# Mixture of experts: a written TensorE order per expert pair, the scatter a pair later, and six of eight gate units inside the pairs

## The chip, the core and the metric

The kernel runs on one core of a Trainium2 chip. The metric is the device time of one execution in microseconds (us); each kernel is run several times and the median is compared. The engines of the core run side by side, each with its own in-order queue: TensorE (PE, matmuls; its weight loads are PEld), VectorE (DVE), ScalarE (ACT), GpSimd (POOL) and SyncE (SP), which here issues nearly all DMA transfers from memory.

## The reference, cut to what matters

Two blocks run on 512 tokens of 1024 features: first two hybrid attention layers with MLPs, then two layers of the second block. The change is in the second half of a layer of the second block:

```python
for i in range(2):
    mix = even_mixer(x, ...) if i % 2 == 0 else odd_mixer(x, ...)
    x = layer_norm(ALPHA * x + mix @ w_o[i], ln1_g[i], ln1_b[i])
    ffn = expert_choice_moe(x, router_w[i], w1[i], w3[i], w2[i])
    ple = sigmoid(x @ ple_gate_w[i] + ple_gate_b[i]) * (p[i] @ ple_w[i])
    x = layer_norm(ALPHA * x + ffn + ple, ln2_g[i], ln2_b[i])

def expert_choice_moe(x, router_w, w1, w3, w2):   # 16 experts, 64 tokens each
    aff = softmax(x @ router_w)                   # 512 x 16
    gates, idx = top_k(aff.T, 64)
    xg = x[idx]                                   # gather
    hid = silu(xg @ w1) * (xg @ w3)               # w1, w3: 1024 x 1024 per expert
    ye = (hid @ w2) * gates
    return zeros.at[idx].add(ye)                  # scatter
```

All of it is float32. The weights of the experts are 16 x 3 x 4 MB per layer, about 200 MB, and each is used once.

## The kernel before, in words

`K.program` runs the layers; `moe` (L1401) is the second half of a layer of the second block. It first multiplies by w_o, normalizes, and computes the routing (`route_tile`, then `choose`: eight rounds of maximum and replace on DVE, and a running count that gives each token its slot, slT). Beside `choose`, TensorE computes gate units. A gate unit (`ple_unit`, L1571) is 128 of the 1024 features of the ple term: 24 matmuls of the gate (pg), 6 of ple_w (pv), a tanh on ACT, a multiply on DVE, four transposes (pt). Its gate weights are loaded as float32 and split in a high and a low part (whi by ACT, wlo by DVE or POOL). Four units run early, their results wait in the tiles `early`; the other four run later, two in pair 1 and two in pair 2.

`experts` (L1604) handles the 16 experts in 8 pairs. One-hot matrices (OH, of four experts, that is two pairs) come from slT. A gather is 64 matmuls of the token features with OH, for two pairs at once. For each pair, each half (512 columns) of w1 and w3 gives two products a1 and a3 (`pair_product`): 8 matmuls in the program, 16 instructions in the trace (float32 goes in two passes), on half of the array for each expert (128 rows x 64 columns), with two weight chunks of 1 MB. Then silu and multiply (ACT, DVE), four transposes of the hidden half (ht), transposes of the affinities (ot), and four products with w2 (y). yh and yl are the split of y times the gate; the scatter is 16 matmuls (sc) in 8 tiles, each added to the tokens by DVE.

Each pair loads 24 chunks of 1 MB. They go through a ring of slots: three in the pool `wr`, five in r1. A slot is loaded again when the products that read it are done; a late gate weight also takes a slot, until it is split. When the late units are over, their memory (`xfp`, `ple`, `wh`) is closed and a pool r2 of 7 slots (layer 0) or 6 (layer 1) is opened over it, before pair 3. Matrix sizes give the memory per partition: xf 2 x 16 KB, pT 2 x 4 KB, early 4 x 2 KB, then the pool `ple` 6 KB (pw, pwh, pwl, pz) and `wh` 8 KB; r2 is 8 KB per slot.

At the start of pair 0 the tokens are scaled by ln1's gain and bias on POOL (`ln_half`, L1541, tiles lnh): four rows, two tags of one buffer.

The order on each engine is not the program's. A scheduler places the instructions with its own estimate of times, by priority and readiness, and adds the semaphores; each engine and each DMA queue then runs its list in order. So before, TensorE's list mixes the products of one pair with the scatter, the gather, the units and the next pair's products.

PSUM has eight banks: two for a1/a3 (tag a), two for y, two for sc, one each for t (ht, ot) and ga.

## Time and profile before

| | us |
|---|---|
| median of 3 runs | 3537.59 (3535.84 to 3539.7) |
| the profiled execution | 3527.1 |
| its span, first to last instruction | 3525.3 |
| TensorE busy in the span | 3346.5 (95%) |
| DVE / ACT / POOL busy | 1579.2 / 1071.5 / 524.3 |

The profile is one execution of the kernel. Busy time of TensorE is from a model of when matmuls end, and overlaps with waiting, so 95% is not a measure of how near the engine is to its peak. The page cuts the span in 40 slices of 88 us; the two expert stages are slices 25 to 30 and 35 to 40.

### The profile page before, as it was taken

The numbers are of one execution on the slowest core, as the hardware profiler recorded it, in microseconds if no ns is written. First come the engines' busy times: TensorE is split into PE (matmuls) and PEld (weight loads), VectorE is DVE, ScalarE is ACT, GpSimd is POOL, SyncE is SP. The second block draws the span as 40 slices with busy tenths as digits, with TensorE's granted clock in tenths as the row PEclk, the third lists the DMA queues.
The fourth block names the chain that finished last, engine by engine and source line by source line (L and its number), as shares of the span: only waits on it lengthen the run. The fifth ranks groups of instructions, "written<-read, shape, count | busy, mean of one in ns | idle before, by whom it ended". The sixth has DMA issues, their size and how long they took to land. (4 is left out here: it accounts for less than half of the span.)

```text
span 3525.3 us, 37543 instructions
## 1 busy us (share of the span) xinstructions
PE 3346.5 (95%) x15018; PEld 2137.7 (61%) x15018; DVE 1579.2 (45%) x2516; ACT 1071.5 (30%) x1937; POOL 524.3 (15%) x368
## 2 busy tenths in 40 slices
PE   8999999999999999999989789999997998999997
PEld 6666588888766658888856774443335667344332
DVE  6555463445555546344567752122116765112213
ACT  4343333223443333322365431111003543111011
POOL 2012120002001212001221323000003203200001
PEclk9999999999999999999989889999998999999999
DMA  5111032333211103233220226999992113889997
GB/s 182 48 37 59 26 108 87 99 101 124 72 60 37 48 28 104 93 98 96 78 76 3 72 109 264 379 373 421 421 402 79 37 38 117 362 340 421 421 421 297
DMA packets 221279, 584.84 MB, mean 166 GB/s; under 512 B 17328, under 2 KB 158000, under 8 KB 169904
## 3 DMA queue, kind: packets, MB, share of 16 engines
q1 hardware_dynamic: 220672, 581.66, 43.6%
q8 instruction: 118, 1.93, 0.2%
q10 hardware_dynamic: 432, 0.79, 0.1%
q14 instruction: 57, 0.47, 0.0%
HBM read 580.30 MB, written 2.10 MB: 165 GB/s over the span
## 5 line engine op out<-in xcount | busy, mean ns | idle before, releaser
L218 ACT CAST whi<-w 128x1024 fp32r<-128x1024 f32 (+1 forms) x312 | 311.1, 1003 | 733.6 <-PE mm L228 502.0
L1631 PE MATMUL a<-w,xg 128*64 128x512 f32 x2048 | 488.1, 597 | 20.4 <-DMA w<-in_w_dram 17.8
L227 PE MATMUL mm<-h,whi 128*128 128x512 f32 x1056 | 415.9, 394 | 4.6 <-ACT whi L218 4.2
L229 PE MATMUL mm<-h,wlo 128*128 128x512 f32 x1056 | 416.6, 395 | 0.1
L228 PE MATMUL mm<-l,whi 128*128 128x512 f32 x1056 | 414.0, 392 | 0.0
L221 DVE TENSOR_TENSOR wlo<-w,whi 128x1024 fp32r<-128x1024 f32 (+1 forms) x234 | 300.3, 1287 | 211.4 <-ACT whi L218 208.3
L1631 PEld LDWEIGHTS a<-w,xg 128*64 128x64 f32 x2048 | 151.5, 136 | 305.7 <-issue 262.3
L221 POOL TENSOR_TENSOR wlo<-w,whi 128x1024 fp32r<-128x1024 f32 x78 | 173.6, 2228 | 782.9 <-ACT whi L218 688.9
L1631 PE MATMUL y<-w,hT 128*64 128x512 f32 x1024 | 268.2, 599 | 0.0
L227 PEld LDWEIGHTS mm<-h,whi 128*128 128x128 f32 x1056 | 199.4, 189 | 49.7 <-ACT whi L218 5.4
L228 PEld LDWEIGHTS mm<-l,whi 128*128 128x128 f32 x1056 | 199.2, 189 | 46.1 <-issue 0.7
L229 PEld LDWEIGHTS mm<-h,wlo 128*128 128x128 f32 x1056 | 199.3, 189 | 44.2 <-DVE wlo L221 1.0
L602 DVE TENSOR_REDUCE mx<-s 128x1 f32<-128x128 f32 x192 | 93.2, 488 | 190.7 <-PE s L601 189.9
L1631 PEld LDWEIGHTS y<-w,hT 128*64 128x64 f32 x1024 | 76.3, 136 | 136.0 <-issue 128.4
L604 ACT ACTIVATE P<-s,mx 128x128 f32<-128x128 f32 x192 | 100.9, 527 | 174.7 <-DVE mx L602 162.4
L1689 DVE SCALAR_TENSOR_TENSOR th<-th,a 128x512 f32<-128x512 f32 x32 | 22.0, 688 | 291.5 <-ACT th L1688 291.4
L1726 DVE TENSOR_TENSOR xtok<-xtok,sc 128x512 f32<-128x512 f32 x128 | 83.5, 683 | 151.7 <-PE sc L1724 151.7
L948 POOL TENSOR_TENSOR u<-u 128x512 f32<-128x512 f32 x64 | 66.6, 1040 | 521.3 <-ACT E L947 275.5
L1697 POOL TENSOR_TENSOR og<-OH,aff 128x512 f32<-128x512 f32 x16 | 16.8, 1048 | 679.4 <-PE ot L1700 662.8
L959 DVE TENSOR_TENSOR y<-mm,r 128x512 f32<-128x512 f32 x64 | 44.2, 690 | 160.8 <-PE mm L229 160.8
L1688 ACT ACTIVATE th<-a 128x512 f32<-128x512 f32 x32 | 19.1, 597 | 319.1 <-PE a L1631 319.1
L227 PE MATMUL mm<-E,whi 128*128 128x512 f32 x256 | 99.7, 389 | 0.0
(584 smaller groups left out, 6286.8 us busy)
## 6 DMA issues: line engine op xcount, KB each, us to landing
w<-in_w_dram SPq DMA_DIRECT2D x384, 1024.0 KB, 16.8
w<-in_w_in_dram SPq DMA_DIRECT2D x32, 1024.0 KB, 5.3
w<-in_w_up_dram SPq DMA_DIRECT2D x32, 1024.0 KB, 5.5
w<-in_w_down_dram SPq DMA_DIRECT2D x32, 1024.0 KB, 5.1
w<-in_w_out_dram SPq DMA_DIRECT2D x8, 1024.0 KB, 5.0
w<-in_w_o_dram SPq DMA_DIRECT2D x8, 1024.0 KB, 4.7
w<-in_ple_gate_w_dram SPq DMA_DIRECT2D x8, 1024.0 KB, 5.2
w<-in_w_in_even_dram SPq DMA_DIRECT2D x7, 1024.0 KB, 5.5
```

Of the source, the lines that this page charges most:

```text
L218: nc.scalar.copy(h, view)
L221: e.tensor_sub(l, view, h)
L227: mm(ps, wh, xh, start=first, stop=False)
L228: mm(ps, wh, xl, start=False, stop=False)
L229: mm(ps, wl, xh, start=False, stop=last)
L602: nc.vector.tensor_reduce(mx[:, i:i + 1], s[:, :n], axis=X, op=OP.max, negate=True)
L604: nc.scalar.activation(pv, s[:, :n], AF.Exp, bias=mx[:, i:i + 1], accum_out=sums[:, i:i + 1])
L948: nc.gpsimd.tensor_mul(u, u, u)
L959: nc.vector.tensor_mul(y, ps, r2)
L1631: nc.tensor.matmul(ps[64 * a:64 * a + 64], lhs(a, 4 * kc + k), cw[a][:, k], start=kc == 0 and k == 0, stop=kc == 1 and k == 3)
L1689: nc.vector.scalar_tensor_tensor(th, th, 1.0, a1, op0=OP.add, op1=OP.mult)
L1726: nc.vector.tensor_add(xs, xs, ps)
```

## The change

TensorE's instructions of the expert stage get a dependency each on the one before (`keep_order`), so that their order is the program's. In the program, a pair now is: the products with w1 and w3 of both halves; then one block with the transposes of the first hidden half and of og, the first gate unit, the scatter of the pair before (`left`), the unit's transposes, the second unit, in pairs 1, 3 and 5 the gather of the next two pairs, the transposes of the second hidden half and of the second unit; then the products with w2. Only two gate units run early, and pairs 1 to 3 have two each; r2 opens at pair 4. yh, yl, oT and the lnh tags get two buffers, and og and ogT share one. The last pair scatters its first half before the last two chunks' products. The ring's slots are taken in the order two of `wr`, five of r1, one of `wr`.

```diff
...
             self.pT = [fp.tile([128, 2, T], F32R, name=f"pT{a}") for a in "hl"]
-            early = [fp.tile([128, T], F32, name=f"pe{m}") for m in range(4)]
+            early = [fp.tile([128, T], F32, name=f"pe{m}") for m in range(2)]
             with ExitStack() as e2:
...
                         self.side_input(l, p, pp)
-                        pgs = [self.gate_load(self.wr, l, i) for i in range(2)]
+                        pg = self.gate_load(self.wr, l, 0)
                     for t in range(4):
...
                         for m in range(4):
-                            self.ple_unit(l, p, pp, m, pgs[m // 2], "wo", "t", early[m])
+                            if m < 2:
+                                for _ in self.ple_unit(l, p, pp, m, pg, ("wo", "wo"), early[m]):
+                                    pass
                             for h in range(2):
...
+    def keep_order(self, first):
+        nc, tc = self.nc, self.tc
+        prev = None
+        for i in nc.cur_bb.bb.instructions[first:]:
+            if i.engine == nc.tensor.engine:
+                if prev is not None:
+                    tc.add_manual_dep(i, prev.name, mybir.DependencyInfo(mybir.DependencyClass.NoSync, mybir.DependencyReason.DATA),
+                                      reason="keep_order")
+                prev = i
     def ln_half(self, p, l, h, *names):
...
         for a, name in zip("gb", names):
-            t = p.tile([128, 512], F32, name="lnh", tag=name)
+            t = p.tile([128, 512], F32, name="lnh", tag=name, bufs=2)
             nc.sync.dma_start(t, bcast(I[f"ln1_{a}_2"][l][512 * h:512 * h + 512], [[0, 128], [1, 512]]))
...
-    def ple_unit(self, l, p, pp, m, pg, tag, tag2, z=None):
+    def ple_unit(self, l, p, pp, m, pg, tags, z=None):
...
         XF = [[self.xf[a][:, k] for k in range(8)] for a in range(2)]
-        ps = pp.tile([128, T], F32, name="pg", tag=tag)
+        ps = pp.tile([128, T], F32, name="pg", tag=tags[0])
         self.proj(ps, pg[:, :, s], *XF, pool=early)
-        pv = pp.tile([128, T], F32, name="pv", tag=tag)
+        pv = pp.tile([128, T], F32, name="pv", tag=tags[1])
         h, lo = [p.tile([128, 2, 128], F32R, name=f"pw{a}") for a in "hl"]
...
         if not early:
-            z = p.tile([128, T], F32, name="pz")
+            z = p.tile([128, T], F32, name="pz", bufs=1)
         nc.scalar.activation(z, ps, AF.Tanh, scale=0.5, bias=self.pb[:, m:m + 1])
...
             nc.vector.scalar_tensor_tensor(z, z, 1.0, pv, op0=OP.add, op1=OP.mult)
-        pt = pp.tile([128, 4, 128], F32, name="pt", tag=tag2)
+        yield
+        pt = pp.tile([128, 4, 128], F32, name="pt", tag="t", bufs=2 if early else 1)
         for t in range(4):
             nc.tensor.transpose(pt[:, t], z[:, 128 * t:128 * t + 128], C["ident"])
-        if not early:
+        if early:
+            nc.scalar.copy(z.rearrange("p (t f) -> p t f", t=4), pt)
+        else:
             nc.vector.tensor_add(xs, xs, pt)
-            return
-        nc.scalar.copy(z.rearrange("p (t f) -> p t f", t=4), pt)
+        yield
...
             self.wh = ef.enter_context(self.pool("wh", 1, side="right"))
-            cyc = [self.wr] + [r1] * R1 + [self.wr] * 2
+            cyc = [self.wr] * 2 + [r1] * R1 + [self.wr]
             self.nch = 0
...
+            def one_hot(grp):
+                OH = p.tile([128, 4, 4, 64], F32R, name="OH")
+                nc.vector.tensor_tensor(OH, slT[:, :, 4 * grp:4 * grp + 4, None].to_broadcast([128, 4, 4, 64]),
+                                        slot[:, None, None, :].to_broadcast([128, 4, 4, 64]), op=OP.is_equal)
+                return OH
             def gather(xg, OH, k2s):
...
                 for k2 in k2s:
-                    ps = pp.tile([128, 2, 256], F32, name="ga", tag="ga", bufs=1) if grp or k2 % 2 == 0 else pp.tile([128, 2, 256], F32, name="ga", tag="y")
+                    ps = pp.tile([128, 2, 256], F32, name="ga", tag=("ga", "y")[k2 % 2], bufs=1 + k2 % 2)
                     for kk in range(2):
...
+            def hidden(th, half, hT):
+                ps = pp.tile([128, 4, 128], F32, name="ht", tag="t", bufs=1)
+                for k in range(4):
+                    nc.tensor.transpose(ps[:, k], th[:, 128 * k:128 * k + 128], C["ident"])
+                nc.scalar.copy(hT[:, 4 * half:4 * half + 4], ps)
+            def scatter(oT, ys, halves, last=False):
+                for half in halves:
+                    yh, yl = ys[half]
+                    for t in range(4):
+                        ps = pp.tile([128, T], F32, name="sc", tag=("y", "sc")[t // 2])
+                        ts_ = slice(128 * t, 128 * t + 128)
+                        nc.tensor.matmul(ps, oT[:, ts_], yh, start=True, stop=False)
+                        nc.tensor.matmul(ps, oT[:, ts_], yl, start=False, stop=True)
+                        xs = x[:, t, 512 * half:512 * half + 512]
+                        nc.vector.tensor_add(xs, xs, ps)
+                        if last:
+                            self.ln_stats(p, st[:, t], x[:, t], half)
+                            if half and l == 0:
+                                self.ln_norm(p, st[:, t], x[:, t])
+            first = len(nc.cur_bb.bb.instructions)
+            OH = one_hot(0)
+            xg = p.tile([128, 8, 256], F32, name="xg")
+            gather(xg, OH, range(2))
+            left = None
             for pi in range(8):
                 grp, pr = divmod(pi, 2)
-                if pi == 3:
+                if pi == 4:
                     ef.close()
...
                         G, Bb = self.ln_load(es.enter_context(self.pool("lng", 1, side="right")), l, "ln2")
-                if pr == 0:
-                    OH = p.tile([128, 4, 4, 64], F32R, name="OH")
-                    nc.vector.tensor_tensor(OH, slT[:, :, 4 * grp:4 * grp + 4, None].to_broadcast([128, 4, 4, 64]),
-                                            slot[:, None, None, :].to_broadcast([128, 4, 4, 64]), op=OP.is_equal)
-                    xg = p.tile([128, 8, 256], F32, name="xg")
-                    gather(xg, OH, range(2))
                 e0 = 2 * pi
+                og = p.tile([128, 4, 2, 64], F32, name="og")
+                nc.gpsimd.tensor_mul(og, OH[:, :, 2 * pr:2 * pr + 2], aff[:, :, e0:e0 + 2, None].to_broadcast([128, 4, 2, 64]))
+                if pr and pi < 7:
+                    OH = one_hot(grp + 1)
                 hT = p.tile([128, 8, 128], F32, name="hT")
+                ths = []
                 for half in range(2):
...
                     for kc in range(2):
-                        if pr == 0 and half == 0 and kc == 1:
+                        if pi == half == 0 and kc == 1:
                             gather(xg, OH, range(2, 4))
...
                                     nc.gpsimd.tensor_add(xs, xs, Bb)
-                                for m in range(4) if h == 0 else ():
+                                for m in range(2) if h == 0 else ():
                                     xs = x[:, :, 128 * m:128 * m + 128]
...
                     nc.vector.tensor_mul(th, th, a3)
-                    ps = pp.tile([128, 4, 128], F32, name="ht", tag="t", bufs=1)
-                    for k in range(4):
-                        nc.tensor.transpose(ps[:, k], th[:, 128 * k:128 * k + 128], C["ident"])
-                    nc.scalar.copy(hT[:, 4 * half:4 * half + 4], ps)
-
-                og = p.tile([128, 4, 2, 64], F32, name="og")
-                nc.gpsimd.tensor_mul(og, OH[:, :, 2 * pr:2 * pr + 2], aff[:, :, e0:e0 + 2, None].to_broadcast([128, 4, 2, 64]))
+                    ths.append(th)
+                units = []
+                if 0 < pi < 4:
+                    pg = self.gate_load(slot_pool(), l, pi)
+                    units = [self.ple_unit(l, plp, pp, 2 * pi + i, pg, ("sc", ("sc", "y")[i])) for i in range(2)]
+                hidden(ths[0], 0, hT)
                 ps = pp.tile([128, T], F32, name="ot", tag="t", bufs=1)
...
                 gate = p.tile([128, 1], F32, name="gate", bufs=2)
-                ogT = p.tile([128, T], F32, name="ogT", tag="th", bufs=2)
+                ogT = p.tile([128, T], F32, name="ogT", tag="og")
                 nc.scalar.activation(ogT, ps, AF.Copy, scale=0.5, accum_out=gate)
-                oT = p.tile([128, T], F32R, name="oT")
+                oT = p.tile([128, T], F32R, name="oT", bufs=2)
                 nc.vector.tensor_scalar(oT, ogT, 0.0, None, op0=OP.is_gt)
+                for u in units[:1]:
+                    next(u)
+                if left:
+                    scatter(*left, range(2))
+                for u in units:
+                    next(u)
+                if pr and pi < 7:
+                    xg = p.tile([128, 8, 256], F32, name="xg")
+                    gather(xg, OH, range(4))
+                hidden(ths[1], 1, hT)
+                for u in units[1:]:
+                    next(u)
                 if pi == 7:
                     self.exp_ln_table()
+                ys = []
                 for half in range(2):
-                    if pi in (1, 2) and half == 0:
-                        pg = self.gate_load(slot_pool(), l, pi + 1)
-                        for m in (2 * pi + 2, 2 * pi + 3):
-                            self.ple_unit(l, plp, pp, m, pg, "sc", "sc")
                     y = pp.tile([128, T], F32, name="y", tag="y")
...
                         pair_product(y, w2, e0, lambda a, k: hT[:, k, 64 * a:64 * a + 64], half, kc)
-                    yh = p.tile([128, T], F32R, name="yh")
-                    yl = p.tile([128, T], F32R, name="yl")
+                        if pi == 7 and half and kc == 0:
+                            scatter(oT, ys, range(1), True)
+                    yh = p.tile([128, T], F32R, name="yh", bufs=2)
+                    yl = p.tile([128, T], F32R, name="yl", bufs=2)
                     nc.scalar.activation(yh, y, AF.Copy, scale=gate)
                     nc.vector.scalar_tensor_tensor(yl, y, gate, yh, op0=OP.mult, op1=OP.subtract)
-                    for t in range(4):
-                        ps = pp.tile([128, T], F32, name="sc")
-                        ts_ = slice(128 * t, 128 * t + 128)
-                        nc.tensor.matmul(ps, oT[:, ts_], yh, start=True, stop=False)
-                        nc.tensor.matmul(ps, oT[:, ts_], yl, start=False, stop=True)
-                        xs = x[:, t, 512 * half:512 * half + 512]
-                        nc.vector.tensor_add(xs, xs, ps)
-                        if pi == 7:
-                            self.ln_stats(p, st[:, t], x[:, t], half)
-                            if half and l == 0:
-                                self.ln_norm(p, st[:, t], x[:, t])
+                    ys.append((yh, yl))
+                left = oT, ys
+            scatter(*left, range(1, 2), True)
+            self.keep_order(first)
             if l == 1:
...
```

## Rows read from the trace of the kernel before

**Rows 1.** The page: span, and the rate of the transfers in 40 slices.
```profile
span 3525.3 us, 37543 instructions
...
GB/s 182 48 37 59 26 108 87 99 101 124 72 60 37 48 28 104 93 98 96 78 76 3 72 109 264 379 373 421 421 402 79 37 38 117 362 340 421 421 421 297
```

**Rows 2.** Windows of both stages: length, engines' busy time, PEclk, DMA share, GB/s.
```profile
2138.70:2647.80 509.10, 483.15 (x2144) 198.33 (x2144) 101.93 (x153) 55.42 (x97) 35.60 (x29) 1.00 0.95 389
2995.30:3502.20 506.90, 486.92 (x2144) 198.53 (x2144) 101.79 (x153) 55.48 (x97) 35.67 (x29) 1.00 0.94 389
```

**Rows 3.** Windows of 50 us, those with late gate units.
```profile
2250.00:2300.00 50.00, 50.00 (x216) 23.20 (x217) 12.11 (x19) 4.42 (x8) 0.00 (x0) 1.00 0.77 308
2300.00:2350.00 50.00, 49.41 (x227) 23.55 (x224) 10.17 (x14) 7.51 (x12) 3.40 (x2) 1.00 0.92 374
...
3100.00:3150.00 50.00, 50.00 (x214) 24.48 (x213) 11.13 (x17) 6.35 (x11) 1.05 (x1) 1.00 0.87 347
3150.00:3200.00 50.00, 48.51 (x227) 24.60 (x227) 11.20 (x15) 7.39 (x12) 1.05 (x1) 1.00 0.85 352
```

**Rows 4.** Chain of waits at layer 0's first gather: start, us, what.
```profile
2120.99 0.35 PE slp L1538 x4
...
2137.43 1.23 DVE OH L1663
2138.70 4.10 PE ga L1642 x32
```

**Rows 5.** Timeline of TensorE, layer 1: start, us, instruction, [idle before].
```profile
2977.47 0.42 PE L1538 MATMUL slp<-c_ident,cum 16*128 16x16 f32 x4
...
2995.29 0.38 PE L1642 MATMUL ga<-OH,xkh 128*128 128x256 f32 x1 [0.48 <-DVE OH L1663]
```

**Rows 6.** Timeline of DVE, layer 0, after the slots' transposes.
```profile
2121.38 0.22 DVE L1539 TENSOR_SCALAR slT<-slp 128x64 f32<-128x64 f32 x1 [2.34 <-PE slp L1538]
```

**Rows 7.** Timeline of the SP queue, start of both stages.
```profile
2149.89 0.33 SPq L1547 DMA_DIRECT2D lnh<-in_ln_b_dram  x1
2152.18 44.25 SPq L1623 DMA_DIRECT2D w<-in_w_dram  x22
...
3008.76 2.05 SPq L1623 DMA_DIRECT2D w<-in_w_dram  x4
```

**Rows 8.** The loads of expert weights: issue to landing.
```profile
DMA to landing us min/median/max: 4.7/16.8/21.2
```

**Rows 9.** Timeline of TensorE: uncut products, transposes, a cut product.
```profile
2155.11 10.52 PE L1631 MATMUL a<-w,xg 128*64 128x512 f32 x48
2165.56 0.66 PE L1693 MATMUL ht<-c_ident,th 128*128 128x128 f32 x4
...
2190.30 1.07 PE L1631 MATMUL y<-w,hT 128*64 128x512 f32 x2
```

**Rows 10.** Timeline of TensorE: an early unit's first matmul, and what follows the unit.
```profile
2113.75 0.50 PE L227 MATMUL pg<-xfh,whi 128*128 128x512 f32 x1 [1.59 <-ACT pe L1593]
...
2120.93 0.42 PE L1538 MATMUL slp<-c_ident,cum 16*128 16x16 f32 x4
```

**Rows 11.** TensorE's waits in the first stage: total us, times, longest.
```profile
PE ot L1700 <- ACT hT L1694: 2.3, 3, 0.8
```

**Rows 12.** DVE operations of scatter and unit: ns minimum, median, maximum.
```profile
L1726 DVE TENSOR_TENSOR xtok<-xtok,sc x61: 672/686/689, 2192.3 to 2650.0; 128x512 f32<-128x512 f32 x61
...
L1595 DVE SCALAR_TENSOR_TENSOR pz<-pz,pv x4: 680/686/687, 2250.8 to 2340.5; 128x512 f32<-128x512 f32 x4
```

**Rows 13.** First loads into r2: layer 0's timeline, layer 1's wait of SP.
```profile
2346.22 0.60 PE L1598 MATMUL pt<-c_ident,pz 128*128 128x128 f32 x4
...
2346.85 2.85 SPq L1623 DMA_DIRECT2D w<-in_w_dram  x6
...
SPq L1623 <- PE pg L229: 6.7, 1, 6.7
```

## The prediction, made before the change was run

> **What bounds the kernel now.** I read the page's time slices first, then the windows of the two expert stages, then the chain of waits, and last the timelines of the SP queue and of TensorE. The slices [rows 1] show the transfer rate at 421 GB/s wherever the experts run: nothing in the kernel moves faster. A weight chunk is 1024 KB, so at that rate one lands every 2.49 us. From the first gather to the last w2 product a stage takes 509.1 us (layer 0) and 506.9 us (layer 1), at a mean of 389 GB/s [rows 2]: transfers fill 92% of it. TensorE is busy in 483 us of 509 too, but much of that is waiting that overlaps: a pair needs 24 chunks, 59.8 us of transfers, while its 12 products take 12 x 3.5 = 42 us (48 instructions, three products, in 10.52 us [rows 9]). So the end of a stage is the start of its stream of chunks, plus the chunks, plus the time in which the stream stands still. It stands still where the ring of eight slots is full and TensorE frees none. In the windows [rows 3] the rate falls to 308 and 374 GB/s in layer 0 and to 347 and 352 in layer 1, all while the four late gate units run: (113 + 47) x 50 / 421 = 19.0 us lost in layer 0, (74 + 69) x 50 / 421 = 17.0 us in layer 1. From the fourth pair on, with six or seven more slots, it is level.
>
> **The change, part by part.** All times below are from the first gather, for one layer.
>
> *Two early units fewer.* The slots' transposes (slp) start at 2120.99, slT follows at 2121.38 [rows 4, 6], but the first gather starts at 2138.70, after two more units and an OH of 1.23 us placed behind the last unit's DVE operation [rows 4]. With two units, DVE does slT (0.22), perhaps one unit operation (0.69 [rows 12]) and OH (1.23): the gather starts near 2123.5, 15.2 us earlier. Layer 1: slp at 2977.47, gather at 2995.29 [rows 5], the same. OH covers the memory of the early units' split weights, which are read by then. Bounds: 13 us (OH late by another unit operation and its transposes) to 16. Taken: -15.2 us.
>
> *Second copies of the scale rows (lnh).* Today the SP queue stands behind the second pair of lnh loads, which wait for GpSimd, until 2149.89; the ninth chunk is issued at 2152.18, and at 3008.76 in layer 1 [rows 7], 13.5 us after the gather. With two buffers nothing waits there: the ninth chunk goes when the first product is done, at 4.1 (gather [rows 4]) + 0.5 + 3.65 = 8.3 us. That is -5.2 us. If ACT's scaling or the queue's order still held it, 0.
>
> *One more gate chunk and one more ple_w* in the stage: 2.49 + 0.6 = +3.1 us of transfers.
>
> *The block.* TensorE now runs, after a pair's sixteen chunks of w1 and w3, all full-width work before w2. I follow the stream by index, gate chunks included. Chunk 8 lands at 8.3 + 4.7 (shortest landing [rows 8]) = 13.0. The second half of the first gather holds a release back by 1.6. Then one chunk per 2.49: chunk 39, the last of pair 1's w1 and w3, lands at 91.8, and its product ends at 95.4, TensorE waiting for data until then. From there to the first freed w2 slot:
> - transposes of the first hidden half, wait for ACT's copy, transposes of og: 0.6 + 0.8 + 0.6 = 2.0 [rows 9, 11]
> - unit 0, gate and ple products: 2113.75 to 2120.93, 7.2 [rows 10]
> - scatter of the pair before, until unit 1 can start: 16 matmuls take 3.6, but a bank comes back only after its DVE addition, and unit 1 wants the bank that the seventh addition frees: 0.8 + 0.69 (the unit's own operation) + 7 x 0.69, about 6.4 [rows 12]; bounds 3.6 and 9
> - unit 1: 7.2; gather, in pairs 1 and 3: 64 matmuls, 2 x 4.0 = 8.0
> - second hidden half, its copy, unit 1's transposes: 2.0; the first w2 product: 3.7
>
> That is 36.5 us with a gather and 28.5 without. In this time the queue can fill eight slots, 19.9 us, and no more. Pair 1: freed at 131.9, chunk 49 lands at 136.6 instead of 91.8 + 10 x 2.49 + 0.6 = 117.3: the stream stands 19.3 us. Pair 2: its sixteenth chunk lands at 136.6 + 37.4 = 174.0, product done at 177.6, freed at 206.1, landing at 210.8 instead of 199.5: 11.3. Pair 3: last chunk at 248.2, done at 251.8. Here the new pool r2 gives slots before w2 does. It lies over the units' memory. Before, layer 0's r2 (56 KB) reached into the pool of pz, and its first load went out at 2346.85, as unit 3's transposes of pz ended (2346.22 + 0.60); layer 1's r2 (48 KB) stopped short of it and waited only for the gate product [rows 13]. With early cut by 4 KB, r2 reaches into that pool in both layers. So I take the wait for unit 1's transposes, which now stand behind the gather: 251.8 + 36.5 - 3.7 = 284.6, landing at 289.3 instead of 273.7: 15.6. If the first slots wait for the gate product alone: 251.8 + 2.0 + 7.2 + 6.4 + 5.7 + 4.7 = 277.8, so 4.1. Together 1.6 + 19.3 + 11.3 + 15.6 = 47.8 us of standing (36.3 with the earlier r2), against 19.0 and 17.0 today.
>
> From pair 4 on fifteen slots hold 37 us of transfers, and a block without units lasts some 18 us: level, as today. The tail after the last chunk keeps its parts.
>
> *Fewer changes of array shape.* A cut product costs TensorE more: two instructions took 1.07 us where 2/48 of the uncut stretch is 0.44 [rows 9]. Most such cuts go; in a stage that waits for chunks this is worth nothing, and I count 0. The Trainium skill (TensorEngine Tiling (Array Packing), Key Properties) says that a change of tiling mode drains TensorE; the trace agrees with the 1.07, and by the rule alone the change would be a gain. The Trainium skill (Perfetto Trace Analysis, Optimization Strategy) also says that regimes with different limits may be worth interleaving; the block takes such interleaving out, and by that rule the sum is the one I forecast.
>
> **The sum.** Layer 0: -15.2 - 5.2 + 3.1 + 47.8 - 19.0 = +11.5; layer 1: +13.5. Together +25 us. The profiled execution took 3527.1 us (span 3525.3), 10.5 less than the median of the runs, 3537.59; the difference is added to the median: **3563 us**, slower by 0.7%.
>
> **Rivals.**
> - *r2 opens at the gate product* (chance 0.25). For: layer 1 did so before. Against: r2 now reaches pz's pool in both. 11.5 less per layer: +2 us, 3540 us; one layer of the two gives 3551.
> - *The written order doesn't keep products out of the block* (0.20): the scheduler still places w2 products or the next pair's between the parts, so slots come free all the time. For: today's order does so, and loses only 19 and 17 us with four units in two pairs, and six units in three pairs are the same density. Against: the dependency is made from each TensorE instruction to the one before. It decides if w2 products stand between unit 0 and unit 1. Then the standing is today's: -15.2 - 5.2 + 3.1 = -17.3 per layer, 3503 us, faster.
> - *The block is longer still* (0.13): each PSUM and split wait in it 3 us more (unit 1's weight split behind the scatter's additions on DVE, the copy of hT behind a cast on ACT). Three blocks and two layers: +18 us, 3581 us.
>
> **How the numbers follow.** The forecast itself has 0.42; its own range, with the scatter's wait between its bounds (-2.8 and +2.6 in six blocks) and the two smaller terms, is 3546 to 3579. The 80% range takes in the rivals to both sides: 3503 to 3582. About 0.2%, 7 us, is what a measurement of this kernel can tell from no change. Faster: 0.20 and 0.05 of the second case; same: the other 0.20 of it; slower: 0.42 + 0.13.
>
> **What would show it.** In the changed profile: the first gather about 2.6 us after slp; no SP wait at lnh; w1/w3 products and w2 products in two unbroken runs per pair; in pairs 1 to 3 the DMA rate near zero for some 19, 11 and 16 us while pg, sc and ga run; the first r2 load at the end of the third pair's last pt; 421 GB/s from then on. I am wrong if the rate stays near 421 through the units, or if r2 loads go out before pt.

## The result, and the profile after

The changed kernel takes 3560.56 us (median of 4 runs, 3558.39 to 3563.05), the kernel before 3537.89 us beside it (4 runs, 3535.84 to 3539.7): ratio 1.0064, 95% interval 1.0047 to 1.0082. Predicted were 3563 us, slower by 0.7%. The profiled execution took 3562.32 us. The page of after, to hold against [rows 1]: span, and the rate in 40 slices.

```profile
span 3560.5 us, 37540 instructions
...
GB/s 180 48 36 55 31 107 83 97 104 124 69 60 36 48 36 97 99 100 95 66 76 13 70 110 389 314 369 387 420 375 61 24 55 183 393 298 330 422 421 291
```

The dent below 421 in each layer is deeper than before (down to 314 and 298, before 373 and 340), and takes three slices instead of two.

*Start of the stage.* TensorE's timeline of after, both layers, and the SP queue (SPq) at the lnh loads and at layer 0's ninth chunk, in the views of [rows 5, 7] (start, us, instruction):

```profile
2126.97 0.42 PE L1540 MATMUL slp<-c_ident,cum 16*128 16x16 f32 x4
...
2129.34 0.39 PE L1664 MATMUL ga<-OH,xkh 128*128 128x256 f32 x1 [0.66 <-DVE OH L1652]
...
2990.31 0.42 PE L1540 MATMUL slp<-c_ident,cum 16*128 16x16 f32 x4
...
2992.68 0.39 PE L1664 MATMUL ga<-OH,xkh 128*128 128x256 f32 x1 [0.66 <-DVE OH L1652]
```
```profile
2100.71 0.44 SPq L1560 DMA_DIRECT2D lnh<-in_ln_b_dram  x1
...
2138.91 0.33 SPq L1639 DMA_DIRECT2D w<-in_w_dram  x1
```

The gather starts 2.37 us after slp in both layers (predicted 2.6; before 17.8 in both, by the same view). The fourth lnh load is out before slp; the ninth chunk goes 9.57 us after the gather (predicted 8.3, before 13.5).

*The block.* TensorE from the last w1/w3 product of pair 1 to its w2 products, and the SP queue's first load into a slot that w2 freed:

```profile
2224.96 3.65 PE L1647 MATMUL a<-w,xg 128*64 128x512 f32 x14 [1.32 <-DMA w<-in_w_dram]
2228.54 0.66 PE L1676 MATMUL ht<-c_ident,th 128*128 128x128 f32 x4
...
2230.40 0.48 PE L227 MATMUL pg<-xfh,whi 128*128 128x512 f32 x1
...
2240.39 0.50 PE L1685 MATMUL sc<-yh,oT 128*128 128x512 f32 x1 [0.59 <-DVE xtok L1688]
...
2243.38 0.50 PE L227 MATMUL pg<-xfh,whi 128*128 128x512 f32 x1 [0.62 <-DVE xtok L1688]
...
2252.12 0.38 PE L1664 MATMUL ga<-OH,xkh 128*128 128x256 f32 x1 [0.68 <-DVE xg L1670]
...
2262.90 0.66 PE L1613 MATMUL pt<-c_ident,pz 128*128 128x128 f32 x4 [0.69 <-ACT hT L1677]
2263.49 13.95 PE L1647 MATMUL y<-w,hT 128*64 128x512 f32 x64
```
```profile
2267.16 0.33 SPq L1639 DMA_DIRECT2D w<-in_w_dram  x1
```

From 2228.61 (2224.96 + 3.65) to 2267.16 are 38.6 us; 36.5 were predicted. There 13.0 us lie between the starts of the two units (2230.40 and 2243.38; predicted 7.2 + 6.4 = 13.6). The gather stands between unit 1 and the second hidden half; in the same timeline it starts at 2250.32 and ends 11.3 us later (predicted 8.0), with a wait of some 0.65 us for DVE at each of its four steps. In pair 2 the block is 27.2 us, from 2314.09 to 2341.32 in the same two timelines (predicted 28.5). The runs of a and y products are unbroken: the order is kept. What the stream loses (its standing) is read from windows of 50 us of after, one per block, layer 0 and then layer 1 (length, engines' busy time, PEclk, DMA share, GB/s; the view of [rows 3]):

```profile
2229.00:2279.00 50.00, 44.69 (x232) 28.84 (x232) 14.12 (x23) 8.42 (x15) 3.46 (x2) 1.00 0.57 231
2329.00:2379.00 50.00, 45.10 (x200) 18.97 (x200) 5.74 (x9) 3.56 (x6) 0.00 (x0) 1.00 0.80 328
2379.00:2429.00 50.00, 42.64 (x218) 28.26 (x220) 13.53 (x21) 8.28 (x14) 3.48 (x2) 1.00 0.90 368
3093.00:3143.00 50.00, 45.62 (x232) 28.95 (x234) 14.11 (x23) 8.00 (x15) 1.05 (x1) 1.00 0.57 233
3193.00:3243.00 50.00, 43.89 (x199) 18.63 (x198) 5.30 (x9) 3.56 (x6) 0.00 (x0) 1.00 0.79 324
3243.00:3293.00 50.00, 43.22 (x218) 28.14 (x220) 14.12 (x22) 8.27 (x14) 1.05 (x1) 1.00 0.68 274
```

At (421 - rate) x 50 / 421 that is 22.6, 11.0 and 6.3 us of standing in layer 0, 22.3, 11.5 and 17.5 in layer 1; predicted 19.3, 11.3 and 15.6 in both. Pair 3 of layer 0 is the one that came out otherwise. What the SP queue waited for there, and its loads into r2, layer 0 and then layer 1 (waits: total us, times, longest):

```profile
SPq L1639 <- PE pt L1613: 10.7, 1, 10.7
SPq L1639 <- POOL wlo L221: 10.5, 1, 10.5
SPq L1639 <- PE pg L229: 9.3, 1, 9.3
...
2408.98 1.94 SPq L1639 DMA_DIRECT2D w<-in_w_dram  x3
...
2423.39 0.33 SPq L1639 DMA_DIRECT2D w<-in_w_dram  x1
```
```profile
SPq L1639 <- PE pt L1613: 12.2, 1, 12.2
SPq L1378 <- PE pg L229: 10.5, 1, 10.5
...
3287.14 1.28 SPq L1639 DMA_DIRECT2D w<-in_w_dram  x3
```

Both layers wait for the gate product and then for pt (the wait for wlo comes ahead of both, for the slot that the gate weight holds). In layer 0 six r2 slots are loaded between the two waits, from 2408.98 on, and pt holds back the seventh alone, until 2423.39; in layer 1 only the two scale rows (L1378) go in between, and every r2 slot stands behind pt, until 3287.14. The reading of this: one slot of r2 lies over pz in each layer, and it is the last of seven to be used in layer 0 and the first of six in layer 1. The profile doesn't show addresses; e1 below tries it.

*The sum, by the traces.* From slp to the end of the last w2 product, in us, of each kernel's one trace, with the median of its runs and their ratio to the kernel before on the same chip (each is described below):

| kernel | layer 0 | layer 1 | median | ratio, 95% interval |
|---|---|---|---|---|
| before | 526.9 | 524.7 | 3537.89 | |
| after | 537.1 | 546.6 | 3560.56 | 1.0064 (1.0047 to 1.0082) |
| e1_swap | 536.7 | 536.7 | 3553.53 | 1.0049 (1.0035 to 1.0063) |
| e2_mixed | 527.4 | 526.3 | 3533.31 | 0.9989 (0.9981 to 0.9998) |
| e3_free | 524.5 | 528.2 | 3530.95 | 0.9993 (0.9985 to 1.0002) |
| e4_early_alone | 528.4 | 524.6 | 3537.07 | 1.0003 (0.9994 to 1.0012) |
| e5_units_0_to_2 | 520.8 | 524.0 | 3518.91 | 0.9958 (0.9946 to 0.9971) |
| e6_units_2_2_1_1 | 522.4 | 525.2 | 3526.41 | 0.9972 (0.9962 to 0.9981) |
| e7_seven_slots | 547.3 | 557.1 | 3585.68 | 1.0142 (1.0129 to 1.0156) |
| e8_before_four_lnh | 528.5 | 526.1 | 3534.78 | 0.9995 (0.9985 to 1.0005) |
| e9_early_scatter_pair7 | 518.8 | 522.6 | 3522.36 | 0.9954 (0.9940 to 0.9967) |
| e10_units_0_to_2_free | 518.9 | 516.5 | 3516.51 | 0.9946 (0.9934 to 0.9959) |
| e11_two_passes | 520.5 | 517.3 | 3513.18 | 0.9941 (0.9927 to 0.9954) |

The change makes the stages 10.2 and 21.9 us longer (predicted 11.5 and 13.5). The spans of the two traces differ by 35.2: 6.1 more lie ahead of layer 0's slp, 3.4 less between the stages, 0.5 more behind. The 6.1 need not be the change's: e8_before_four_lnh, the same as before up to there, reaches slp 9.4 us later than before did (last section). So 29 us by the traces stand against 22.7 by the medians; the two profiled executions don't settle the last 6 us. In e8, whose one edit shows no effect on the time, the two stages come out 3.0 us longer than in before, so a difference of 1 or 2 us between two stages of the table says nothing.

### The profile page after: what moved, and what is told of

Its sections match the earlier page's. It is cut to its first block, busy times and chain, and to the rows that moved or that the text cites. A ratio compares the mean times of both kernels' runs of the same rounds, so it can differ in the third digit from the quotient of the medians.

```text
span 3560.5 us, 37540 instructions
## 1 busy us (share of the span) xinstructions
PE 3297.3 (93%) x15018; PEld 2148.4 (60%) x15018; DVE 1585.0 (45%) x2527; ACT 1068.8 (30%) x1933; POOL 509.2 (14%) x357
## 5 line engine op out<-in xcount | busy, mean ns | idle before, releaser
L1647 PE MATMUL a<-w,xg 128*64 128x512 f32 x2048 | 469.6, 596 | 86.2 <-DMA w<-in_w_dram 86.2
L218 ACT CAST whi<-w 128x1024 fp32r<-128x1024 f32 (+1 forms) x312 | 311.1, 1004 | 729.7 <-PE mm L228 503.4
L1647 PE MATMUL y<-w,hT 128*64 128x512 f32 x1024 | 226.1, 594 | 2.6 <-DMA w<-in_w_dram 2.6
L1778 DVE SCALAR_TENSOR_TENSOR yl<-y,gate,yh 128x512 fp32r<-128x512 f32 x32 | 24.0, 751 | 204.1 <-ACT yh L1777 204.1
## 6 DMA issues: line engine op xcount, KB each, us to landing
w<-in_w_dram SPq DMA_DIRECT2D x384, 1024.0 KB, 16.2
```

Source lines behind the costliest of these rows:

```text
L218: nc.scalar.copy(h, view)
L1647: nc.tensor.matmul(ps[64 * a:64 * a + 64], lhs(a, 4 * kc + k), cw[a][:, k], start=kc == 0 and k == 0, stop=kc == 1 and k == 3)
```

## The experiments

Two theories are held against each other. A, the prediction's: the stream of chunks stands because no slot comes free in the block, and that is the loss. B: in the pairs with units TensorE has more to do than the chunks need time, and the stand only shows it.

**e1_swap.** Layer 1: which r2 slot lies over pz.
```diff
+                    if l == 1:
+                        G, Bb = self.ln_load(es.enter_context(self.pool("lng", ...)), l, "ln2")
                     r2 = es.enter_context(self.pool("r2", R2 - l, side="right"))
...
-                    if l == 1:
-                        G, Bb = self.ln_load(es.enter_context(self.pool("lng", ...)), l, "ln2")
```


> The changed kernel, with one pair of statements exchanged in layer 1: the scale rows of the last normalisation get their memory before the seven (here six) new chunk slots, so that the slot that lies over the late units' pz is the last of the six to be used and not the first. Theory (the stream of chunks is what the stage waits for): the new slots open at unit 5's gate product, as in layer 0, where pair 3's stand was 4.2 us against 16.0 us in layer 1; the stage of layer 1 gets 11 us shorter (544 to 533) and the kernel goes from 3560.6 to about 3549 us. Rival (TensorE's work in pairs 1 to 3 is the bound, and chunks that come sooner only lie longer): no change, 3558 to 3563 us.

Five of the six r2 loads now go out behind the last unit's gate and ple products, and the sixth alone waits for pt; SP's timeline of e1 (the row of six ends with that sixth load), its wait, and the window of pair 3's block in layer 1:
```profile
3275.30 0.43 SPq L1378 DMA_DIRECT2D lnb<-in_ln_b_dram  x1
3275.82 12.70 SPq L1639 DMA_DIRECT2D w<-in_w_dram  x6
...
SPq L1639 <- PE pt L1613: 9.7, 1, 9.7
```
```profile
3244.00:3294.00 50.00, 43.21 (x218) 28.14 (x220) 14.11 (x22) 8.27 (x14) 1.05 (x1) 1.00 0.89 363
```
363 instead of 274 GB/s, 6.9 us of standing instead of 17.5, and layer 1's stage is 9.9 us shorter, equal to layer 0's. The medians differ by 7.0 us, by the ratios it is 5, and the intervals of the two ratios overlap: it is the trace that shows the price of a slot that waits for pt, some 10 us of the 11 expected, and with it the rival is out.

**e2_mixed.** Still a written order, but w2 products between the units (pairs 1 to 3). Parts of the edit; in these pairs the block's own code is left out.
```diff
...
                     for kc in range(2):
                         pair_product(y, w2, ...)
+                        if mixed and kc == 0:
+                            next(units[half])
+                            if half == 0:
+                                hidden(ths[1], 1, hT)
+                            scatter(*left, range(half, half + 1), tags=("sc", "sc"))
+                            next(units[half])
...
+                if mixed and pr:
+                    xg = p.tile([128, 8, 256], F32, name="xg")
+                    gather(xg, OH, range(4))
```


> The changed kernel, still in a written order, but in pairs 1 to 3 the block is taken apart: first w2 product right behind the first hidden half, then unit, second hidden half, half of the scatter, two w2 products, second unit, other half of the scatter, last w2 product, gather. All products stay uncut; slots now come free 6 us after the last w1/w3 product instead of 27 to 39 us. Theory A (the prediction's: the stream stands because no slot comes free in the block): the stands of pairs 1 and 2 (21.4 and 10.0 us) mostly go, 25 us less per layer, about 3510 us. Theory B (in pairs 1 to 3 TensorE has more to do, about 77, 66 and 77 us per pair by the groups of the changed kernel, than the 63 us that a pair's chunks need; the stand is only where the surplus shows): the chunks come sooner in pair 1 and are late by as much in pair 3; the stages keep their length within 10 us, 3545 to 3580 us.

3533.31 us lies between the two, in neither range. Taking the block apart is worth 27 us of median (9.7 and 20.3 in the stages; about 10 of the latter is what e1 gave). But it ends at the stages of the kernel before, not 25 us per layer below those of after. TensorE's timeline of e2 at pair 2, from the gather on:
```profile
2273.89 25.11 PE L1647 MATMUL a<-w,xg 128*64 128x512 f32 x114
2301.03 3.65 PE L1647 MATMUL a<-w,xg 128*64 128x512 f32 x14 [2.03 <-DMA w<-in_w_dram]
```
Seven products in a row without a wait for data, where after waits from its third on. So theory A fits the block, and theory B fits what is left when it is gone; e7 and e11 try each of them further. The Trainium skill (Perfetto Trace Analysis, Optimization Strategy) says that regimes with different limits may be worth interleaving; these 27 us agree.

**e3_free.** `self.keep_order(first)` is left out, nothing else.

> The changed kernel without the written order: TensorE's instructions are again placed by the scheduler; everything else as changed. Theory A: the written order is not what costs, since in the scheduler's order too the first w2 product of pairs 1 to 3 stands behind both units and most of the gather; 3552 to 3570 us, with TensorE busy longer per stage (the cut products; before the change 484 us with two units fewer, against 471 us). Rival: the strict order's waits (the gather's four of 0.65 us, the scatter's) are the loss, and the scheduler fills them: 3535 to 3545 us. Second rival: the uncut products were worth something, and cutting them again costs more than 10 us: over 3572 us.

My theory A said no change and is wrong: 3530.95 us, 0.9993 against after's 1.0064. Deleting this one line takes back all of the change's loss. The first rival (the strict order's waits) is nearer, but the gain is larger than its range, and the waits are only part of it. The second rival is out. The first w2 product still stands behind both units, but the scheduler has shortened what is ahead of it: the transposes of the first hidden half and of og stand between products of pair 1, half of the scatter behind w2, and the units' matmuls in the gather's waits. SP's first load into a w2 slot, and the window of that block; its last w1/w3 product ended at 2230.33:
```profile
2258.69 0.33 SPq L1639 DMA_DIRECT2D w<-in_w_dram  x1
```
```profile
2230.00:2280.00 50.00, 49.34 (x242) 28.69 (x241) 13.51 (x21) 7.55 (x13) 2.40 (x1) 1.00 0.77 318
```
A block of 28.4 us instead of 38.6, and 12.2 us of standing instead of 22.6: 10.2 and 10.4 less. The stand follows the length of the block one for one: it is the block less 16.2 us here, less 16.0 and 16.2 in pairs 1 and 2 of after.

**e4_early_alone.** The kernel before with two early units and six late ones in pairs 1 to 3, new slots a pair later, free order, old scatter. Part of the edit:
```diff
...
-                    if pi in (1, 2) and half == 0:
-                        pg = self.gate_load(slot_pool(), l, pi + 1)
-                        for m in (2 * pi + 2, 2 * pi + 3):
+                    if pi in (1, 2, 3) and half == 0:
+                        pg = self.gate_load(slot_pool(), l, pi)
+                        for m in (2 * pi, 2 * pi + 1):
```


> The kernel before, with one part of the change alone: two early units instead of four, six late units in pairs 1 to 3, the new slots a pair later; no written order, single lnh buffers, scatter in its old place. Theory B (TensorE's work is the bound while units run): the gather starts about 15 us sooner in each layer, and two more units of 7.2 us each and a third pair with units in an eight-slot ring take it back: 3535 to 3560 us. Theory A (the block of the written order is the loss, the moved units cost only their chunk): the earlier gather is kept, 3508 to 3520 us.

The same as before, as theory B has it: the gather starts 2.5 us after slp, 15.3 sooner, and the stages end at 528.4 and 524.6 from slp instead of 526.9 and 524.7. All of the earlier start is given back within the stage. Whether the two added units take it, or the new slots that come a pair later, this run doesn't separate.

**e5_units_0_to_2.** e2_mixed with e1's exchange, units in pairs 0 to 2, new slots from pair 3. Part of the edit:
```diff
...
-                if pi == 4:
+                if pi == 3:
...
-                if 0 < pi < 4:
-                    pg = self.gate_load(slot_pool(), l, pi)
+                if pi < 3:
+                    pg = self.gate_load(slot_pool(), l, pi + 1)
```


> The kernel of the mixed order (w2 products between the units, all products uncut), with the six late units in pairs 0 to 2 instead of 1 to 3, the new slots from pair 3 on, and the two statements of layer 1 exchanged. Theory B (TensorE's own work bounds pairs 1 to 3: in the mixed order it runs there nearly without a break, while in pair 0 and the first half of pair 1 it stands some 10 us per layer for chunks): units in pair 0 fill that time, and the larger set of slots begins a pair sooner; 5 to 12 us less per layer, 3508 to 3524 us against 3533. Rival (chunks are the bound everywhere, a unit in pair 0 only stops the stream sooner): 3530 to 3537 us.

3518.91 us, faster than both kernels: theory B's range, the rival is out. The run changes three things at once beside e2; e6 says something on which of them it is.

**e6_units_2_2_1_1.** The same with `ms = ((2, 3), (4, 5), (6,), (7,), (), (), (), ())[pi]` for the late units of a pair, new slots from pair 4.

> The same, but with two units in each of pairs 0 and 1, one in pair 2 and one in pair 3 (the fourth gate chunk is loaded twice, 2.5 us more of transfers per layer); new slots from pair 4 on. Theory B: TensorE's surplus over the transfers is spread thinnest, pairs 2 and 3 need about 66 and 70 us instead of 66 and 77 against 63 us of chunks; 10 to 17 us less per layer than the mixed order, 3498 to 3513 us. Rival as in the run before: 3530 to 3540 us.

A gain, but smaller than forecast, in neither range. It is 6 us by the ratios beside e2 (0.9972 against 0.9989), with the new slots no sooner than there and one gate chunk more to load: so not all of e5's gain comes from the earlier slots (e1's exchange is in both). Against e5 it is slower by the ratios, with intervals that overlap; whether the added chunk or the later slots cost it was not tried.

**e7_seven_slots.** after with `R1=4`.

> The changed kernel with a ring of seven slots instead of eight (R1 4 instead of 5), nothing else. Theory A (in the block the queue fills the ring and stops; the trace of the changed kernel and of the one without written order have stands of the block's length less 17.2 us): one slot less is 2.49 us more of standing in each of the three blocks, 15 us in both layers, about 3575 us; a little more (up to 3590) if the last pairs, with one slot less too, no longer hold 421 GB/s. Rival (TensorE's total work is the bound of the changed kernel too): under 5 us, 3560 to 3566 us.

25 us slower than after, and the rival is out. The stages are 10.1 and 10.5 us longer; two windows of the blocks of pairs 1 and 2:
```profile
2233.00:2283.00 50.00, 44.69 (x229) 28.91 (x230) 13.85 (x23) 8.45 (x16) 3.46 (x2) 1.00 0.52 208
2333.00:2383.00 50.00, 43.35 (x194) 18.53 (x194) 8.93 (x15) 3.66 (x6) 0.00 (x0) 1.00 0.74 306
```
25.3 and 13.7 us of standing, 2.7 and 2.6 more than after; a slot is 2.49 us of transfers. The ring is what the stream has to live on during the block. That the stages grow by 20.6 us in all and not by 15 was not followed further.

**e8_before_four_lnh.** The kernel before with four lnh tiles: `self.ln_half(p, l, h, *(("yh", "yl"), ("oT", "og"))[h])`.

> The kernel before with one part of the change alone: four buffers for the lnh rows (the second pair in the memory of oT and og), so that the queue doesn't stand behind GpSimd and the ninth chunk goes out some 5 us sooner. If the stream of chunks is what the stage waits for from its first chunk on: 5 us less per layer, about 3526 us. If TensorE's work in pairs 1 and 2 sets the time at which the stream goes on there, chunks that come sooner are given back: 3533 to 3538 us.

No change, as the second case had it, but for another reason. SP's timeline, with the gather starting at 2148.07:
```profile
2134.42 0.43 SPq L1547 DMA_DIRECT2D lnh<-in_ln_b_dram  x1
...
2161.55 0.80 SPq L1623 DMA_DIRECT2D w<-in_w_dram  x2
```
The lnh loads are out 13.7 us before the gather, and the ninth chunk still goes 13.5 us after it. In e3_free (two buffers, free order) it also goes 13.5 us after. The trace puts the 26.2 us of waiting ahead of that load in e8 down to an a product: it waits for the first product, which the scheduler cuts up with the second half of the gather.

**e9_early_scatter_pair7.** e5 with pair 6's scatter between the halves of pair 7's w1/w3 products.
```diff
+                    if pi == 7 and half:
+                        scatter(*left, range(2))
+                        left = None
```


> The kernel of units in pairs 0 to 2, with one thing moved: the scatter of pair 6 stands between the two halves of pair 7's w1/w3 products, where TensorE waits 1.3 us for chunks at each product, and not behind them, where it holds back the last w2 products. In the changed kernel those products start 6.5 us after the last w1/w3 product and the last one ends 7.4 us after the last chunk, 5.2 us before the change; with 4.4 us of scatter away it should end some 4.4 us after it. If the end of the stage is now set by TensorE behind the last chunk: 3 us less per layer, 3511 to 3515 us. If the last chunk itself comes later for it (the products of pair 7 free their slots later): no change, 3517 to 3522 us.

The stages are 2.0 and 1.4 us shorter than e5's; the ratios (0.9954 and 0.9958) don't tell them apart. Inconclusive.

**e10_units_0_to_2_free.** e5 without `self.keep_order(first)`.

> The kernel of units in pairs 0 to 2 without the written order. The run of the changed kernel without written order came out within 3 us of the mixed written order. If the place of the units decides and the order only has to let slots come free: 3515 to 3524 us, beside 3519. If the mixed written order is worth something of its own once TensorE has time to spare (uncut products, 470 against 484 us busy): 3526 to 3536 us.

3516.51 us, as e5 (the intervals of the ratios overlap): no worth of the mixed written order shows, though TensorE is busy 489.77 us in layer 0 without it and 471.13 with it. Of the kernels that leave nothing out this has the lowest ratio, 0.9946 (0.9934 to 0.9959); e5 and e9 are not clear of it.

**e11_two_passes.** e2_mixed with one of the three products of the split (weights' high part by activations' low part) left out in the late units, where `two` is set. Part of the edit:
```diff
...
         mm(ps, wh, xh, start=first, stop=False)
-        mm(ps, wh, xl, start=False, stop=False)
+        if not self.two:
+            mm(ps, wh, xl, start=False, stop=False)
```


> The mixed order (second run), with one of the three passes left out in the six late units of each layer (the high half of the weights by the low half of the activations): 10 of 30 products of a unit, 2.4 us of 7.25, so 14 us less TensorE work per layer in pairs 1 to 3; splits, loads, order and waits stay. Theory B (in the mixed order TensorE is the bound in pairs 1 to 3): most of the 14 us come back in each layer, stages of 510 to 514 us instead of 525 and 524, about 3505 to 3512 us. Rival (the stream is bound by when slots come free and by the transfers, TensorE's work only fills its waits): under 4 us per layer, 3526 to 3536 us.

6.9 and 9.0 us less per stage, 0.9941 against 0.9989: some half of the 14 us, between the two theories. TensorE's work counts in pairs 1 to 3, but not for all of their length.

The later scatter, the second buffers of yh, yl and oT, the ring's new order and the early scatter of the last pair were not run alone.

## Why the prediction was right, point by point

- *Two early units fewer, -15.2 us*: measured -15.4 and -15.5. The step was right as a term; in e4, with the units moved into pairs 1 to 3 and without the written order, it is worth nothing in the end.
- *lnh, -5.2 us*: the size was near, -3.9 (9.57 instead of 13.5), but the reason was wrong. With lnh out of the way (e8, e3) the ninth chunk still goes 13.5 us after the gather; in after the first product is uncut and frees its slots sooner.
- *The block, 36.5 and 28.5 us*: 38.6 and 27.2. The mechanism is shown twice: the stand follows the block's length (e3) and the ring's size (e7). The scatter's wait came out nearly as taken (13.0 for 13.6). The term that was too small is the gather, 11.3 us for 8.0: the 8.0 had no wait for DVE in it.
- *r2 waits for unit 1's transposes, 15.6 us*: right in layer 1 (17.5), wrong in layer 0 (6.3), where the rival's 4.1 was nearer. The forecast's own sign of being wrong, r2 loads that go out before pt, came true in layer 0. The failed step is "with early cut by 4 KB, r2 reaches into that pool in both layers. So I take the wait for unit 1's transposes". By e1 it does reach there, with one slot, and which slot of the rotation that is decides: six of layer 0's seven r2 loads went out before pt, none of layer 1's.
- *The tail keeps its parts*: it did not quite. In after the last w2 product of layer 0 starts at 2660.46, behind eight scatter matmuls and a wait of 0.78 us on DVE; it ends 7.4 us after the last chunk has landed, 5.2 before.
- *Fewer changes of array shape, 0*: right as far as the runs tell. e10 and e5 differ in `keep_order` alone: TensorE is busy 489.77 us in layer 0 with cut products and 471.13 with uncut ones, and the kernel with cut products is not slower. The Trainium skill (TensorEngine Tiling (Array Packing), Key Properties) says that a change of tiling mode drains TensorE; no run here separates such drains from the rest of the busy time.
- *The sum*: 11.5 and 13.5 against 10.2 and 21.9. Layer 0's missing 9.3 us in pair 3 are made up for the most part by pair 1's block (3.3 us more) and the tail (2.2); layer 1 has those and the full wait. So 3563 against 3560.56 us is nearer than the terms were: the forecast's price for r2 open at the gate product in one layer alone was 3551, and terms that came out larger than taken (pair 1's block, the tail, the ninth chunk) brought it back. That much of the agreement is luck.
- *The rivals*: the second (products stay in the block) didn't happen. Its price was wrong too: without the written order the kernel goes to 3531 us (e3), not 3503. I had six units in three pairs stand like four in two; in e2 and e4 the stages from slp are as long as before, so the earlier gather is given back there. e11 shows that in e2 TensorE's work in those pairs is part of the reason; what the rest is stays open.

TensorE's waits for chunks say the same in one row each: the a products of after and of e2 (busy, mean ns | idle before them, releaser).
```profile
L1647 PE MATMUL a<-w,xg 128*64 128x512 f32 x2048 | 469.6, 596 | 86.2 <-DMA w<-in_w_dram 86.2
```
```profile
L1647 PE MATMUL a<-w,xg 128*64 128x512 f32 x2048 | 462.0, 596 | 48.7 <-DMA w<-in_w_dram 48.6
```
In after TensorE waits 86 us for chunks (both layers), and the chunks wait for TensorE in the blocks: with a ring of eight chunks, 20 us of transfers, the two take turns.

## What to carry to other kernels

A stream through a ring stands for the stretch without a release, less most of what the ring holds (here less 16 us, with a ring of 20); work of another kind belongs between the products that release slots, not in one block ahead of them. An earlier start can be given back by the engine that takes over the moved work (e4: 15 us sooner, no gain): try that work where the engine waits for data (pair 0 in e5, -0.4%, together with the larger set of slots a pair sooner). Where new buffers lie over old ones, see which one of the rotation lies over the tile that is freed last.

## What was not expected of the hardware

The same code takes 9 us longer in some executions, with the clock: an ACT operation (L218) that starts at 460.59 us in before starts at 469.68 in e8, with the same code up to there. Windows of 5 us of the kernel before and of e8_before_four_lnh (the sixth figure behind the length is PEclk):
```profile
210.00:215.00 5.00, 5.00 (x44) 4.75 (x42) 4.93 (x9) 1.70 (x5) 2.39 (x1) 1.00 0.20 36
215.00:220.00 5.00, 5.00 (x23) 2.19 (x23) 2.95 (x7) 2.27 (x7) 0.00 (x0) 1.00 0.50 174
350.00:355.00 5.00, 5.00 (x23) 2.94 (x21) 1.60 (x4) 0.74 (x2) 0.00 (x0) 1.00 0.45 156
```
```profile
210.00:215.00 5.00, 5.00 (x37) 3.87 (x37) 4.89 (x8) 2.23 (x5) 2.37 (x1) 1.00 0.00 0
215.00:220.00 5.00, 5.00 (x23) 3.26 (x21) 3.26 (x7) 2.14 (x7) 0.00 (x0) 0.53 0.70 210
350.00:355.00 5.00, 5.00 (x14) 3.57 (x13) 3.62 (x7) 1.30 (x3) 1.30 (x1) 0.50 0.09 9
```
The granted clock was 0.53 and 0.50 there, nearly all at the lower of the two levels (1.2 of 2.4 GHz), with TensorE busy 5.00 of 5.00 us in the window before it fell at 215 us. The profile of after has it (0.50 from 215 to 220 us), that of before, 10.5 us quicker than its median, does not: part of what two traces differ by can be this, and why the clock falls in some executions and not in others no run here shows. Stage lengths, at a granted clock of 0.99 to 1.00 here, compare better than spans.
